# The low part of a weight as a negated copy and an accumulating DMA: a hybrid attention and state-space layer

## The chip, the cores and the metric

The kernel runs on one core of a Trainium2 chip. The metric is the device time of one execution in microseconds; three executions of the kernel before took 1957.34 to 1957.73 us, median 1957.66.

## What is computed

One layer serves a prompt of 1024 tokens and 8 samples of 16 tokens, 1152 tokens in all, with a model width of 1024. All tensors are float32. Cut to what matters:

```python
mod = jax.nn.silu(c) @ w_ada + b_ada
shift, scale, gate = jnp.split(mod[:, None, :], 3, axis=-1)
h = rms_norm(x, norm_g) * (1 + scale) + shift
proj = h @ w_in                      # q, k, v, z_att, z_ssd, xbc, dt, gates
q, k, v, z_att, z_ssd, xbc, dt_raw, gates = jnp.split(proj, IN_SPLITS, axis=-1)
o_att, k_st, v_st = attn_fn(rms_norm(q), rms_norm(k), v)       # 16 heads of 64, band of 8 chunks
att_branch = (o_att * jax.nn.silu(z_att)) @ w_att_proj
xbc, conv_new = causal_dwconv(xbc, conv_buf, conv_w, conv_b)   # 4 taps, 3072 channels
xs, bm, cm = jnp.split(jax.nn.silu(xbc), ...)
y, h_new = ssd_scan(xs, softplus(dt_raw + dt_bias), -jnp.exp(a_log), bm, cm, h0)   # 32 heads of 64
y = rms_norm_grouped((y + d_skip * xs) * jax.nn.silu(z_ssd))
merged = jax.nn.sigmoid(g_att) * att_branch + jax.nn.sigmoid(g_ssd) * (y @ w_ssd_proj)
out = x + gate * (merged @ w_out)
```

## The kernel before

Channels lie on the 128 partitions and tokens along the free axis, so an activation is a set of tiles of 128 x 1152. A projection is cut into jobs. A plain job has one weight block of 128 x 1024 float32 (eight tiles of 128 x 128, 512 KB) and computes 128 output channels for all tokens, in three groups of 384 tokens.

Matmuls run on float32r operands, and precision is kept by splitting each operand in two: a high part, rounded to float32r, and a low part, what is left of it. For each tile `mm` in `dense` (L436 to L445) gives TensorE three matmuls: high weights by high activations (L442), high by low (L443) and low by high (L445). So the high part of a weight is needed by the first matmul of a job and the low part by the third. A group of tokens has 24 matmuls and accumulates in one PSUM tile; the first two groups take turns in a pool of two (`psd`), in the state-space stage the third has a tile of its own (`pss`).

The weights arrive in order. `w_ahead` (L308) loads the next blocks by SyncE's DMA queue into two raw buffers, as soon as one is free. `w_split` (L316) makes the parts of one block: ScalarE copies the raw block into the high part (L334), VectorE subtracts the high part from the raw block into the low part (L335), and the raw buffer is given back. High and low parts of plain jobs live in four slots of `rarena` (`L_W`), that is two pairs: one for the job that runs and one for the next. `w_next` splits the next job's block while a job runs, if a pair of slots is free; otherwise `w_over` (L394) overwrites the pair of the running job piece by piece (L407, L408).

Jobs are numbered in the order of the weights: 0 to 15 are the attention stage's (`jobs_att[0]` is 16), 16 to 71 the 56 jobs of the state-space stage and its merge gates, and the last 32 (72 to 103) those of the tail: attention projection, state-space projection, output projection.

The state-space stage runs from about 640 to 1540 us of the profiled execution. Beside the dense jobs it has, for each of 16 pairs of heads, the convolution (`conv_gen`, L1229 to L1270), the decay masks (L1441 to L1459) and the scan itself (`main`, L1481 to L1616). ScalarE also evicts PSUM there (L1240, L1355, L1423). GpSimd does small copies and memsets for the convolution (L1232 to L1252), masked copies for the scan (L1515), and starts the DMAs that store results (L1253, L1356, L1540, L1590, L1616). While the attention stage ends, it also does the inverse square roots of its norms (L290 to L296, L960, L964).

The order of work: a Python generator traces the dense matmuls and, paced by a clock of its own, the other streams. A planner then lists each engine's instructions: among those that it expects to be ready it takes the one traced first, except that an instruction given to `keep_in_program_order` (`late` in the code) stays behind what was traced before it on its engine. On the chip each engine then runs its list in order and waits where an operand is not there. `w_split` has a parameter `keep`, which pins both its instructions when the next job is split inside the attention stage's last projections; job 16 is split that way.

Of the kernel before, what the change touches and what calls it, by code (L numbers as in the profile page):

```python
# [9 lines left out]
AF = mybir.ActivationFunctionType  # L10
ALU = mybir.AluOpType
# [110 lines left out]
def trunk_kernel(ctx: ExitStack, tc: tile.TileContext, h):  # L122
    nc = tc.nc
# [105 lines left out]
    def alloc(lay, tag, cols, cold=None):  # L229
        if lay is L_Q:  # L230
            try:
                return alloc(L_QR, tag, cols)
            except NoSlot:
                pass
        if lay is L_SSD and tag == "H":
            try:
                return Buf(qarena, qarena.alloc(L_QS, "ada", cols), cols)
            except NoSlot:
                pass
        if lay is L_Q or lay is L_QS:  # L240
            return Buf(qarena, qarena.alloc(lay, tag, cols), cols)
        if lay is L_W3 or lay is L_W7 or lay is L_VT or lay is L_VA:
            return Buf(varena, varena.alloc(lay, tag, cols), cols)
        if lay is L_H or lay is L_W or lay is L_WA or lay is L_QR or lay is L_ST:
            return Buf(rarena, rarena.alloc(lay, tag, cols, cold), cols)
        if (lay is L_SSD or lay is L_HEAD or lay is L_TAIL) and tag == "T" or lay is L_HEAD and tag == "Y":
            if v_open[0]:
                try:
                    return alloc(L_VT, "T", cols)
                except NoSlot:  # L250
                    pass
        return Buf(arena, arena.alloc(lay, tag, cols), cols)
# [46 lines left out]
    jobs, parts = [], []  # L299
# [8 lines left out]
    def w_ahead():  # L308
        while not hold[0] and loaded[0] < len(parts) and len(wraw) < 2:
            b = alloc(L_RAW, "raw", 1024)  # L310
            x = parts[loaded[0]]
            dma(b.ap[:, :x.shape[1]], x)
            wraw[loaded[0]] = b
            loaded[0] += 1

    def w_split(i, keep=lambda x: x, cold=None):  # L316

        n = len(jobs[i])
        if n == 4:
            return w_split_last(i, keep)  # L320
        if i not in wsplit:
            lay = L_W3 if n == 3 else L_WA if 0 < i < jobs_att[0] else L_W
            hi = alloc(lay, "w", n * 1024, cold)
            try:
                lo = alloc(lay, "w", n * 1024, cold)
            except NoSlot:
                hi.free()
                raise
            wsplit[i] = [hi, lo, 0]
        hi, lo, j = wsplit[i]  # L330
        w_ahead()
        b = wraw.pop(jobs[i][j])
        c = slice(j * 1024, (j + 1) * 1024)
        keep(nc.scalar.activation(hi.r[:, c], b.ap, AF.Copy))  # L334
        keep(nc.vector.tensor_tensor(lo.r[:, c], b.ap, hi.ap[:, c], ALU.subtract))  # L335
        b.free()
        wsplit[i][2] = j + 1
        w_ahead()

    def w_split_last(i, keep):  # L340

        n = NQL
        if i not in wsplit:
            hi = alloc(L_W7, "w", 7 * n)
            wsplit[i] = [hi, alloc(L_W7, "w", 7 * n), 0]
        hi, lo, j = wsplit[i]
        if j == 3:
            row = alloc(L_WA, "w", 1024)
            wsplit[i].append(row)
        w_ahead()  # L350
        b = wraw.pop(jobs[i][j])
        pieces = [(hi.r, hi.ap, lo.r, 2 * j * n, 0, 2 * n if j < 3 else n)]
        if j == 3:
            pieces.append((row.r, row.ap, row.r[:, n:], 0, n, n))
        for h_, f_, l_, o, r, w in pieces:
            keep(nc.scalar.activation(h_[:, o:o + w], b.ap[:, r:r + w], AF.Copy))
            keep(nc.vector.tensor_tensor(l_[:, o:o + w], b.ap[:, r:r + w], f_[:, o:o + w], ALU.subtract))
        b.free()
        wsplit[i][2] = j + 1
        w_ahead()  # L360
# [4 lines left out]
    def get_w(i):  # L365
        while w_left(i):
            w_split(i)
        return wsplit[i][:2]

    def w_wait(i):  # L370
        while w_left(i):
            try:
                w_split(i)
            except NoSlot as x:
                blocked[0] = str(x)
                yield None
        return wsplit[i][:2]

    def w_next(i, keep=lambda x: x):
        if w_left(i + 1):  # L380
            try:
                w_split(i + 1, keep, "q")
            except NoSlot:
                pass
# [37 lines left out]
    jobs_att = [len(jobs)]  # L422
# [99 lines left out]
    for k in range(KT):  # L522
        b = alloc(L_START, "T", NT)
# [200 lines left out]
    for k in range(KT):  # L724
        if k == 0:
# [22 lines left out]
            for i in range(3):  # L748
# [3 lines left out]
                b = wraw[1 + i] = alloc(L_RAW, "raw", 1024) if i < 2 else alloc(L_START, "T", 1024)  # L752
# [1172 lines left out]
```

## Time and profile before

| | |
|---|---|
| median of three runs | 1957.66 us |
| profiled execution, span | 1955.7 us |
| TensorE matmul busy | 1938.3 us, 99% |
| TensorE weight load busy | 1859.4 us, 95% |
| VectorE busy | 1168.5 us, 60% |
| ScalarE busy | 776.4 us, 40% |
| GpSimd busy | 323.5 us, 17% |
| granted TensorE clock | 1.00 in all slices |
| DMA | 238.62 MB, mean 122 GB/s |

The table shows one execution as the hardware profiler saw it. An engine's busy time leaves out what it waits. A matmul's end is modelled, so the share of TensorE says that it was hardly ever without an instruction, not that its array was full. The profile's views used below are the engine table, the chain of work that ended last, the stretch table (busy time of each engine between two times), the list of waits, the groups of instructions by line, the timeline of one engine, and the DMA starts with their time to landing.

### The profile page before, as it was taken

How to read it: one execution, taken by the hardware profiler on the slowest of the kernel's cores; microseconds unless marked ns; L12 is line 12 of the kernel's file. 1: busy time of each engine (PE TensorE's matmuls, PEld its weight loads, DVE VectorE, ACT ScalarE, POOL GpSimd, SP SyncE). 2: the span in 40 equal slices, each digit the busy share in tenths (PEclk: the TensorE clock that was granted, in tenths of full speed). 3: DMA queues.
4: the chain of work that ended last, by engine and by line, in shares of the span. 5: the costliest groups of instructions: out<-in, count | busy, mean ns of one | idle time of the engine just before them, and what ended most of it. 6: DMA issues, size and time to landing. Idle time of an engine off the chain costs nothing.

```text
span 1955.7 us, 35068 instructions
## 1 busy us (share of the span) xinstructions
PE 1938.3 (99%) x14091; PEld 1859.4 (95%) x14091; DVE 1168.5 (60%) x2441; ACT 776.4 (40%) x1589; POOL 323.5 (17%) x624
## 2 busy tenths in 40 slices
PE   7999999999999999999999999999999999999999
PEld 5999999899998999999999999999999999999999
DVE  7455555556555765757566666576674334777732
ACT  8444444445444557344454434345351301111200
POOL 0312213122131201212212221122212100000000
PEclk9999999999999999999999999999999999999999
DMA  9124244232432325433333333332337642331241
GB/s 367 60 81 131 86 132 131 90 122 88 131 112 96 112 88 160 128 112 110 95 132 129 106 103 114 117 118 91 117 118 291 234 140 92 104 104 56 86 143 52
DMA packets 81209, 238.62 MB, mean 122 GB/s; under 512 B 14284, under 2 KB 15320, under 8 KB 81048
## 3 DMA queue, kind: packets, MB, share of 16 engines
q1 hardware_dynamic: 72088, 207.74, 32.7%
q0 software_dynamic: 8960, 28.65, 3.8%
q8 instruction: 111, 1.82, 0.4%
q14 instruction: 50, 0.41, 0.1%
HBM read 192.70 MB, written 43.66 MB: 121 GB/s over the span
## 4 chain that ended last, share of the span: by engine, by line
PE 96%; DVE 1%; ACT 1%; DMA 1%; issue 0%; SPq 0%
PE d L442 13%; PE d L443 13%; PE d L445 13%; PE s L442 5%; PE s L445 5%; PE s L443 5%; PE d L508 5%; PE d L506 5%; PE d L507 5%; PE g L1043 3%; PE g L1066 3%; PE g L1553 2%; PE s L1122 2%; PE g L1526 1%; PE g L1573 1%; PE g L1122 1%
## 5 line engine op out<-in xcount | busy, mean ns | idle before, releaser
L442 PE MATMUL d<-rarena 128*128 128x384 f32 x1520 | 517.4, 340 | 0.3 <-ACT arena L1355 0.3
L445 PE MATMUL d<-rarena 128*128 128x384 f32 x1520 | 511.4, 336 | 0.0
L443 PE MATMUL d<-rarena 128*128 128x384 f32 x1520 | 511.0, 336 | 0.0
L442 PEld LDWEIGHTS d<-rarena 128*128 128x128 f32 x1520 | 285.6, 188 | 4.6 <-issue 2.3
L443 PEld LDWEIGHTS d<-rarena 128*128 128x128 f32 x1520 | 285.6, 188 | 2.8 <-issue 2.4
L445 PEld LDWEIGHTS d<-rarena 128*128 128x128 f32 x1520 | 285.5, 188 | 1.1 <-issue 0.9
L334 ACT ACTIVATE rarena<-arena 128x1024 fp32r<-128x1024 f32 x92 | 97.5, 1060 | 314.1 <-PE s L443 226.2
L442 PE MATMUL s<-rarena 128*128 128x384 f32 x640 | 216.7, 339 | 0.0
L443 PE MATMUL s<-rarena 128*128 128x384 f32 x640 | 214.2, 335 | 0.0
L445 PE MATMUL s<-rarena 128*128 128x384 f32 x640 | 214.1, 334 | 0.0
L508 PE MATMUL d<-va_att,rarena 128*128 128x384 f32 (+1 forms) x559 | 195.0, 349 | 0.0
L506 PE MATMUL d<-va_att,rarena 128*128 128x384 f32 (+1 forms) x559 | 193.9, 347 | 0.0
L507 PE MATMUL d<-va_att,rarena 128*128 128x384 f32 (+1 forms) x559 | 191.0, 342 | 0.0
L335 DVE TENSOR_TENSOR rarena<-arena,rarena 128x1024 fp32r<-128x1024 f32 x92 | 113.2, 1230 | 82.7 <-ACT rarena L334 82.4
L1031 ACT ACTIVATE arena<-arena 128x640 f32<-128x640 f32 (+2 forms) x144 | 101.4, 706 | 138.0 <-DVE arena L1140 99.7
L442 PEld LDWEIGHTS s<-rarena 128*128 128x128 f32 x640 | 120.3, 188 | 1.0 <-issue 1.0
L443 PEld LDWEIGHTS s<-rarena 128*128 128x128 f32 x640 | 120.3, 188 | 0.0
L445 PEld LDWEIGHTS s<-rarena 128*128 128x128 f32 x640 | 120.1, 188 | 0.0
L508 PEld LDWEIGHTS d<-va_att,rarena 128*128 128x128 f32 x559 | 105.5, 189 | 3.9 <-issue 2.7
L1263 DVE SCALAR_TENSOR_TENSOR arena<-arena 128x1176 f32<-128x1176 f32 x66 | 99.9, 1514 | 15.5 <-ACT arena L1260 14.2
L506 PEld LDWEIGHTS d<-va_att,rarena 128*128 128x128 f32 x559 | 105.2, 188 | 3.1 <-issue 1.2
L507 PEld LDWEIGHTS d<-va_att,rarena 128*128 128x128 f32 x559 | 105.2, 188 | 1.0 <-issue 0.4
(345 smaller groups left out, 3212.9 us busy)
## 6 DMA issues: line engine op xcount, KB each, us to landing
arena<-in_wall_dram SPq DMA_DIRECT2D x85, 512.0 KB, 3.9
arena<-in_kc_dram SPq DMA_DIRECT2D x64, 256.0 KB, 4.2
arena<-in_vc_dram SPq DMA_DIRECT2D x64, 256.0 KB, 3.4
arena<-acs_d SPq DMA_DIRECT2D x19, 576.0 KB, 3.8
gate_d<-arena POOLq DMA_DIRECT2D x48, 192.0 KB, 2.5
arena<-y_d SPq DMA_DIRECT2D x15, 576.0 KB, 5.6
arena<-in_wssd_dram SPq DMA_DIRECT2D x16, 512.0 KB, 4.1
arena<-in_wada_dram SPq DMA_DIRECT2D x15, 512.0 KB, 8.9
```

Of the source, the lines that this page charges most:

```text
L334: keep(nc.scalar.activation(hi.r[:, c], b.ap, AF.Copy))
L335: keep(nc.vector.tensor_tensor(lo.r[:, c], b.ap, hi.ap[:, c], ALU.subtract))
L442: nc.tensor.matmul(ps, hi.r[:, wc], kh.r[:, tok], start=k == 0, stop=False)
L443: nc.tensor.matmul(ps, hi.r[:, wc], kl.r[:, tok], start=False, stop=False)
L445: nc.tensor.matmul(ps, lo.r[:, wc], kh.r[:, tok], start=False, stop=k == nk - 1)
L506: nc.tensor.matmul(ps, kh.r[:, tok], wh, start=j == 0, stop=False)
L507: nc.tensor.matmul(ps, kh.r[:, tok], wl, start=False, stop=False)
L508: nc.tensor.matmul(ps, kl.r[:, tok], wh, start=False, stop=j == KT - 1)
L1031: nc.scalar.activation(p, p, AF.Exp, bias=sm_[:, 4 + e:5 + e], scale=-1.0, accum_out=sm_[:, 6 + e:7 + e])
L1043: nc.tensor.transpose(ps[:, s * P:(s + 1) * P], p[:, (j + s) * P:(j + s + 1) * P], ident)
L1122: late(nc.tensor.matmul(banks[k][e][:, o:o + w], x.r[hs, qs], y.r[hs, kk], start=i == 0, stop=i == 2))
L1263: nc.vector.scalar_tensor_tensor(yc, r.ap[:, j:j + n], w4[:, i, j:j + 1], yc, ALU.mult, ALU.add)
```

## The change

In `w_split`, for a block of the state-space stage (jobs 16 to 71), the low part is no longer VectorE's subtraction. ScalarE copies the high part, multiplied by -1, into the low part's slot, and a DMA started from GpSimd's queue adds the weights to it; it reads them from DRAM once more (`parts[...]` is the block that the raw buffer was loaded from). The jobs of the other stages, and the piecewise path in `w_over`, are as before. From here on lines have numbers four higher.

```diff
         keep(nc.scalar.activation(hi.r[:, c], b.ap, AF.Copy))
-        keep(nc.vector.tensor_tensor(lo.r[:, c], b.ap, hi.ap[:, c], ALU.subtract))
+        if jobs_att[0] <= i < len(jobs) - 32:
+            keep(nc.scalar.activation(lo.r[:, c], hi.ap[:, c], AF.Copy, scale=-1.0))
+            keep(nc.gpsimd.dma_start(lo.r[:, c], parts[jobs[i][j]], accum_op=ALU.add))
+        else:
+            keep(nc.vector.tensor_tensor(lo.r[:, c], b.ap, hi.ap[:, c], ALU.subtract))
         b.free()
```

## Rows read from the trace of the kernel before

**Rows 1.** The page: span; busy us (share of the span) and instructions by engine
```profile
span 1955.7 us, 35068 instructions
PE 1938.3 (99%) x14091; PEld 1859.4 (95%) x14091; DVE 1168.5 (60%) x2441; ACT 776.4 (40%) x1589; POOL 323.5 (17%) x624
```
**Rows 2.** The page: the chain that ended last, shares of the span by engine
```profile
PE 96%; DVE 1%; ACT 1%; DMA 1%; issue 0%; SPq 0%
```
**Rows 3.** Stretch table: stretch, length, busy us by engine, clock, DMA share, GB/s
```profile
640.00:1540.00 900.00, 897.53 (x6552) 878.49 (x6551) 578.17 (x1021) 393.78 (x807) 182.56 (x345) 1.00 0.38 126
```
**Rows 4.** Waits of TensorE, 640 to 1540: waiter <- releaser: total us, times, longest
```profile
PE g L1481 <- DVE arena L1269: 1.8, 2, 1.4
...
PE d L442 <- ACT arena L1355: 0.3, 1, 0.3
```
**Rows 5.** Groups by line: form, count | busy us, mean ns | idle before, releaser
```profile
L334 ACT ACTIVATE rarena<-arena 128x1024 fp32r<-128x1024 f32 x92 | 97.5, 1060 | 314.1 <-PE s L443 226.2
...
L335 DVE TENSOR_TENSOR rarena<-arena,rarena 128x1024 fp32r<-128x1024 f32 x92 | 113.2, 1230 | 82.7 <-ACT rarena L334 82.4
```
**Rows 6.** Timeline of ScalarE: start, us, form; high parts of jobs 16, 21, 22, 29, 55, 60
```profile
644.52 1.06 ACT L334 ACTIVATE rarena<-arena 128x1024 fp32r<-128x1024 f32 x1
...
735.09 1.06 ACT L334 ACTIVATE rarena<-arena 128x1024 fp32r<-128x1024 f32 x1 [0.26 <-PE s L443]
...
765.55 1.06 ACT L334 ACTIVATE rarena<-arena 128x1024 fp32r<-128x1024 f32 x1
...
875.57 1.05 ACT L334 ACTIVATE rarena<-arena 128x1024 fp32r<-128x1024 f32 x1
...
1278.28 1.04 ACT L334 ACTIVATE rarena<-arena 128x1024 fp32r<-128x1024 f32 x1
...
1351.59 1.05 ACT L334 ACTIVATE rarena<-arena 128x1024 fp32r<-128x1024 f32 x1
```
**Rows 7.** Timeline of TensorE: the third matmul of the same jobs
```profile
650.14 0.42 PE L445 MATMUL d<-rarena 128*128 128x384 f32 x1
...
757.60 0.35 PE L445 MATMUL d<-rarena 128*128 128x384 f32 x1
...
776.67 0.34 PE L445 MATMUL d<-rarena 128*128 128x384 f32 x1
...
884.42 0.33 PE L445 MATMUL d<-rarena 128*128 128x384 f32 x1
...
1286.12 0.33 PE L443 MATMUL d<-rarena 128*128 128x384 f32 x1
1286.30 0.33 PE L445 MATMUL d<-rarena 128*128 128x384 f32 x1
...
1361.29 0.33 PE L445 MATMUL d<-rarena 128*128 128x384 f32 x1
```
**Rows 8.** DMA starts of GpSimd: count, KB each, median us to landing
```profile
gate_d<-arena POOLq DMA_DIRECT2D x48, 192.0 KB, 2.5
...
out_hs_dram<-qa_ssd POOLq DMA_DIRECT2D x8, 512.0 KB, 2.9
```
**Rows 9.** Line 312, loads of weights of 512 KB, 740 to 1540
```profile
DMA to landing us min/median/max: 3.5/4.1/7.9
```
**Rows 10.** Line 1356, GpSimd's DMA starts, 740 to 1540: ns min/median/max
```profile
L1356 POOL DMA_DIRECT2D gate_d<-arena x45: 539/544/627, 752.5 to 1536.3; - x45
```
**Rows 11.** Timeline of GpSimd, around 646 and 871
```profile
645.91 3.69 POOL L291 TENSOR_TENSOR arena<-arena 128x16 f32<-128x16 f32 x1
...
871.48 0.54 POOL L1590 DMA_DIRECT2D y_d<-arena  x1 [15.50 <-DVE arena L1586]
```
**Rows 12.** Timeline of TensorE, 651 to 659, other work than the projection
```profile
651.01 0.71 PE L1043 MATMUL g<-arena 128*128 128x128 f32 x5
...
653.60 3.50 PE L1066 MATMUL g<-arena 128*64 128x128 f32 x60
...
657.02 1.30 PE L1202 MATMUL g<-arena 128*32 128x128 f32 x40
```

## The prediction

> **What bounds the kernel now.** I read the engine table of the page first. Of a span of 1955.7 us TensorE is busy for 1938.3, 99%; VectorE for 1168.5 and ScalarE for 776.4 [rows 1]. The chain that ended last agrees: 96% of it is TensorE, 1% VectorE [rows 2]. These are means over stages, so the second view is the stretch table of the stage that is changed. From 640 us, where the stage's first projection falls, to 1540 us TensorE is busy for 897.53 of 900.00 us [rows 3]. The reader is to see two things there. All idle time of TensorE in the stage is 900.0 - 897.5 = 2.5 us, so that is the most that relief on any other engine can give back. And nothing but TensorE is near its limit: VectorE has 578 of 900 us, ScalarE 394, GpSimd 183. The view of waits names what ended that idle time: VectorE's L1269 with 1.8 us, in two waits; ScalarE's eviction L1355 with 0.3 us, in one [rows 4]. The subtraction L335 is not among the releasers.
>
> The profiled execution stands 2.0 us under the median (1957.66 - 1955.7): what lies around the span. I sum on the span and add that.
>
> **The change, part by part.** Jobs are numbered as in the code; 16 to 71 are in the new branch. Jobs 17 to 19 take the other path (w_over), which keeps VectorE, so 53 jobs change.
>
> Removed: 53 subtractions at 1230 ns [rows 5], 65 us of VectorE. TensorE doesn't wait for them, so this is worth what part of the 2.5 us of idle time they caused: between -2.5 and 0. I take 0, because ScalarE's new copy stands at the same points of the same stretches.
>
> Added on ScalarE: 53 copies. The nearest row is the copy of the same size that makes the high part, 1060 ns [rows 5]: 56 us, which brings ScalarE in the stage from 394 to about 450 of 900 us. Behind each copy stand on ScalarE the evictions of PSUM, and for those TensorE waits. The cover is the second PSUM buffer of the projections: a group is 24 matmuls, whose starts are 0.17 us apart (1286.12 to 1286.30 [rows 7]), about 4.1 us, and an eviction that starts 1.1 us later still ends inside that. Without that cover the price would be 53 x 1.06 = 56 us; with it, 0 to 2 us. I take 0.5, since the one eviction in the waits is late by 0.3 us only [rows 4].
>
> Added on GpSimd's queue: 53 DMA starts. A start there takes 0.54 us, at most 0.63 [rows 10], 29 us in all on an engine with 183 of 900. The start waits for ScalarE's copy, and behind it are queued the stores (L1253, L1356, L1540, L1590, L1616), the halo memsets and copies, and the masks L1515 for TensorE's L1598. As the copy follows the high part directly, they wait about 1 us more; none of them releases TensorE in the waits [rows 4]. Cost: 0. On SP's queue nothing is added; the raw buffer is freed by the high part alone, so the next load may start some 1.2 us earlier. That is worth nothing, as no projection waits for it.
>
> The price that decides is the landing of the accumulating DMA, because now the low part is ready when it has landed. The trace shows no such DMA. Below: a plain store of 512 KB from GpSimd's queue lands in 2.9 us, median [rows 8]. Above: the slowest load of 512 KB of these weights from SP's queue lands in 7.9 us; its median is 4.1 us [rows 9]. The DMA has this load's bytes to fetch and 512 KB of the low part to read as well. From 192 KB in 2.5 us to 512 KB in 2.9 us, a store costs 0.4 us per 320 KB [rows 8], so the second read is about 0.6 us. I take 4.1 + 0.6 = 4.7 us, near the median load, and keep 2.9 and 7.9 (with the second read about 8.5) for the range.
>
> For the adding in the DMA the Trainium skill has a rule, in "Collectives: The Full Stack", section "The bandwidth ceiling: the fold count and why AG ≠ RS ≠ AR": a transfer that adds reads two sources through one ring and so runs at half the rate of a copy. By it the landing would be at most twice the median load, an estimate of 8.2 us, and the sum that of the first rival at its far end. No run here shows it yet.
>
> How long may it take? The end of the high part (L334) against the third matmul of the job (L445, the first that needs the low part) gives each job's room. For 49 of the 53 jobs it is 10.1 us or more: job 22 has 776.67 - 766.61 = 10.1, job 21 with 757.60 - 736.15 = 21.5 the most [rows 6, 7]. This is by construction: the high part waits for the slots that the job before the last one held (most of ScalarE's idle time ahead of L334, 226.2 us, ended with TensorE's L443 [rows 5]) and so starts as the job before begins. From the room go 1.06 us for the copy and up to 0.6 us for an instruction that runs on GpSimd just then: 8.4 us and more are left, against 4.7. They cost nothing. Four jobs have less [rows 6, 7]:
> job 55: 1286.30 - 1279.32 = 7.0, left 5.3; job 29: 884.42 - 876.62 = 7.8, left 6.1; job 60: 1361.29 - 1352.64 = 8.7, left 7.0. All three above 4.7. If one of them meets the slowest landing it costs 1 to 3 us; I take 0.4 for the three.
> Job 16: 650.14 - 645.58 = 4.6. Its copy would end at 646.7, but GpSimd is then in the power step L291 from 645.91 for 3.69 us [rows 11], so the DMA starts at 649.6 and lands at 654.3: 4.2 us after TensorE's need.
>
> Whether these 4.2 us are lost depends on the planner, which lists TensorE's instructions by what it expects to be ready. If it sees the late landing it can list other work first; L1043 (0.71) and L1202 (1.30) follow in 651 to 658, and L1066 with 3.50 as soon as its copies are there [rows 12]. Ends: 0 and 4.2. I take that the first two are moved, 2.0 us, and 2.2 are lost.
>
> Sum: 0 (VectorE) + 0.5 (evictions) + 0.4 (three tight jobs) + 2.2 (job 16) = +3.1 us. Span 1958.8, time 1960.8.
>
> **The rivals.** (1) Job 16 uncovered, landing 5 to 8 us. The mechanism is one wait of TensorE on the DMA at the stage's first projection, with the three tight jobs behind it. At 5 us it costs 4.5 and nothing else: 1962. At 8 us: 7.5 + 2.7 + 1.9 + 1.0 = 13: 1971. It is slower from the point where more than 3.9 us stay uncovered. For it: GpSimd is really busy there for 3.69 us, and the pinned order of this one job leaves the DMA no way past. Against it: other TensorE work stands right behind.
> On a delay of the start the Trainium skill says, in "SBUF — State Buffer", section "Who interferes with whom", that VectorE in its two-port modes locks GpSimd out while it writes descriptors, and that queues like SP's don't suffer. It speaks against moving this work from VectorE to GpSimd's queue; by it some landings would be later by one VectorE instruction, which is a time inside this rival. The trace doesn't show it: with VectorE busy for 64% of the stage [rows 3], 45 starts lie between 0.539 and 0.627 us [rows 10].
> (2) The add runs far below the copying rate, landing 10 us or more. Then the ordinary jobs pay too: 24 of 53 have less than 13 us of room. At 10 us I sum some 25 us over nine jobs, time 1983; at 12 us some 56, 2013. For it: no row shows what an add costs. Against it: 10 us is over twice the median load.
> (3) Head of GpSimd's queue. A start that the planner lists behind a store waits with it; the store of y at 871 stood there for 15.50 us [rows 11]. A job with 8.4 us left would lose 7. Two to four of these: 1972 to 1985. Against it: the listed order has been near to what happened in every stage, with TensorE never waiting.
> (4) All is hidden and VectorE's relief gives back the idle time: up to -2.5, 1955.2 to 1957.7. It can hardly go past that, as TensorE's own work is the same.
> That the change doesn't do what it says: only if the planner kept L335 for these jobs, which the branch rules out; three jobs of 56 are outside.
>
> **How the numbers follow.** A measurement of this kernel can tell about 0.2%, 3.9 us, from no change: from 1953.7 to 1961.6 is "the same". Forecast 1960.8 (own range 1957.7 to 1961.6): 0.46. Rival 1: 0.30. Rival 2: 0.10. Rival 3: 0.06. Rival 4: 0.08, of which 0.03 for an order of TensorE's work that happens to be better by more than 0.2%. So faster 0.03, same 0.51, slower 0.46. The range takes in the forecast, rival 1, half of rival 3 and rival 4 but for its tail: 1955.5 to 1978, leaving out about 0.16.
>
> **What would show it.** L335 on rarena falls from 92 to 39 instructions; a second ScalarE row of 1060 ns follows L334; GpSimd has 53 DMA rows into rarena of about 0.55 us. Landing of these: median 4.7 right, 8 rival 1, 10 rival 2. TensorE's waits on a DMA into rarena: one of 0 to 4 us near 650 by the forecast; 5 to 8 there, and near 884, 1286 and 1361, by rival 1; many of 1 to 4 through the stage by rival 2; a few of 5 or more after a long GpSimd wait by rival 3. I would be wrong in the cover if TensorE stays 99.9% busy with landings of 8 us and more, and in the 0 for VectorE if its idle time goes down.

## The result and the profile after

The changed kernel took 1961.34 us, median of 8 executions (1959.05 to 1965.93); the kernel before, measured beside it, 1957.5 us (1956.1 to 1958.33). The ratio is 1.0023, 95% interval 1.0013 to 1.0034. The profiled execution has a span of 1959.5 us against 1955.7 [rows 1].

The page of the changed kernel, engine table and chain of work that ended last, answers to [rows 1, 2]:

```profile
span 1959.5 us, 35155 instructions
...
PE 1940.4 (99%) x14091; PEld 1860.7 (95%) x14091; DVE 1103.7 (56%) x2388; ACT 823.1 (42%) x1642; POOL 347.3 (18%) x677
...
PE 91%; DMA 4%; issue 2%; ACT 2%; DVE 1%; POOL 0%; SPq 0%; POOLq 0%; ACTq 0%
```

The exchange itself is as written: VectorE has 53 instructions fewer and 65 us less, ScalarE and GpSimd 53 more each. In the chain DMA went from 1% to 4% and TensorE from 96% to 91% [rows 2]. The stretch table of the stage and TensorE's waits in it answer to [rows 3, 4]:

```profile
640.00:1540.00 900.00, 895.15 (x6526) 875.35 (x6525) 512.36 (x968) 439.79 (x859) 204.59 (x395) 1.00 0.58 156
```

```profile
PE d L449 <- DMA rarena<-in_wall_dram: 4.3, 4, 3.1
PE g L1485 <- DVE arena L1273: 0.5, 1, 0.5
```

TensorE's idle time in the stage went from 2.5 to 4.9 us, and its makeup is another: four waits of the third matmul (L449, before L445) on the new DMA, the longest 3.1 us, and 0.5 us on L1273, where L1269 (now L1273) with 1.8 us and L1355 with 0.3 us stood before. Two columns at the end of the stretch table show the second fetching of the 53 blocks: DMA share 0.58 for 0.38, 156 GB/s for 126. The DMA issues on the page, and the view of line 337 (duration of its starts, and issue to landing):

```profile
rarena<-in_wall_dram POOLq DMA_DIRECT2D x53, 512.0 KB, 6.7
```

```profile
L337 POOL DMA_DIRECT2D rarena<-in_wall_dram x53: 873/900/1078, 648.5 to 1526.9; - x53
...
DMA to landing us min/median/max: 5.4/6.7/11.4
```

A landing takes 6.7 us, median, and a start 0.90 us against 0.54 for a store [rows 10]. TensorE's timeline gives the other three waits on it, at jobs 29, 60 and 70; the longest, at job 55, stands further down:

```profile
881.48 0.44 PE L449 MATMUL d<-rarena 128*128 128x384 f32 x1 [0.45 <-DMA rarena<-in_wall_dram]
...
1365.26 0.44 PE L449 MATMUL d<-rarena 128*128 128x384 f32 x1 [0.66 <-DMA rarena<-in_wall_dram]
...
1524.86 0.44 PE L449 MATMUL d<-rarena 128*128 128x384 f32 x1 [0.18 <-DMA rarena<-in_wall_dram]
```

**Where the time went.** Setting the starts of the jobs of both traces side by side gives the ledger. Up to job 16 the changed kernel is 0.3 us ahead. Between job 16 and job 25 (650 to 821 us) it gains 3.3 us: all the idle time that TensorE had there before is gone, and some more. These are the first matmuls of the two jobs, before (L442) and after (L446):

```profile
649.76 0.33 PE L442 MATMUL d<-rarena 128*128 128x384 f32 x1
...
824.58 0.33 PE L442 MATMUL d<-rarena 128*128 128x384 f32 x1
```

```profile
649.51 0.34 PE L446 MATMUL d<-rarena 128*128 128x384 f32 x1
...
821.03 0.33 PE L446 MATMUL d<-rarena 128*128 128x384 f32 x1
```

Then it loses: 0.7 at job 29, 0.7 at job 50 (with the wait of L1485, 0.5 us), 4.9 at job 55, 0.95 at job 60, 0.45 at job 70. Together -0.3 - 3.3 + 7.7 = +4.1, and the spans differ by +3.8; the rest is gained behind job 72.

Job 55 is more than half of the loss. Its way can be followed on three engines. ScalarE's timeline (high part L334, negated copy L336):

```profile
1275.78 1.04 ACT L334 ACTIVATE rarena<-arena 128x1024 fp32r<-128x1024 f32 x1
1276.73 0.68 ACT L1457 ACTIVATE va_ssd<-va_ssd,arena 128x128 f32<-128x128 f32 x2
1277.32 0.36 ACT L1247 ACTIVATE arena<-s 128x256 f32<-128x256 f32 x1
1277.58 0.26 ACT L1248 ACTIVATE arena<-s 128x128 f32<-128x128 f32 x1
1277.74 1.27 ACT L1457 ACTIVATE va_ssd<-va_ssd,arena 128x128 f32<-128x128 f32 x4
1278.91 1.05 ACT L336 ACTIVATE rarena<-rarena 128x1024 fp32r<-128x1024 f32 x1
1279.86 1.36 ACT L1264 ACTIVATE arena<-arena 128x1176 f32<-128x1176 f32 x1
```

GpSimd's timeline, the start of the DMA, and TensorE's, the second and the third matmul of the job:

```profile
1281.55 0.90 POOL L337 DMA_DIRECT2D rarena<-in_wall_dram  x1 [2.54 <-ACT arena L1264]
```

```profile
1284.10 0.34 PE L447 MATMUL d<-rarena 128*128 128x384 f32 x1
1287.50 0.69 PE L449 MATMUL d<-rarena 128*128 128x384 f32 x1 [3.06 <-DMA rarena<-in_wall_dram]
```

The high part ends at 1276.82; the copy starts 2.1 us later, behind the eight other instructions of four rows; it ends at 1279.96; the DMA starts 1.6 us after that, in the trace behind ScalarE's L1264; it lands 5.90 us later, at 1287.45, and TensorE goes on at 1287.50. And the wait has a tail. The stretch table of what follows (its last columns: granted clock, DMA share, GB/s):

```profile
1287.50:1290.00 2.50, 2.50 (x8) 2.50 (x9) 1.74 (x3) 2.50 (x4) 0.31 (x2) 0.50 0.30 82
1290.00:1293.00 3.00, 3.00 (x17) 3.00 (x16) 0.16 (x1) 0.50 (x1) 0.88 (x1) 0.87 0.89 331
```

From the end of the wait of 3.06 us TensorE was granted 0.50 of its clock, 1.2 of 2.4 GHz, until about 1290.8 (0.87 in the second stretch is 0.8 us at 0.50 and the rest at 1.00). That isn't idle time in any view: 8 matmuls in 2.50 us, where 0.17 us apiece [rows 7] would have given 14. Half of 3.3 us is 1.6 us, and 3.1 + 1.6 = 4.7 is the 4.9 of the ledger but for 0.2. A stretch of 3.4 us at half clock takes about 0.001 from the mean clock of an execution of 1960 us. Of the eight executions only the shortest (1959.05 us) has a mean of 1.000, the profiled one and four others 0.999 and two 0.998; so most of them, but not all, seem to have such a stretch. Where it lies in the others no profile shows.

### The profile page after: what moved, and what is told of

It is laid out like the page before. It is cut to its first block, busy times and chain, and to the rows that moved or that the text cites. A ratio compares the mean times of both kernels' runs of the same rounds, so it can differ in the third digit from the quotient of the medians.

```text
span 1959.5 us, 35155 instructions
## 1 busy us (share of the span) xinstructions
PE 1940.4 (99%) x14091; PEld 1860.7 (95%) x14091; DVE 1103.7 (56%) x2388; ACT 823.1 (42%) x1642; POOL 347.3 (18%) x677
## 4 chain that ended last, share of the span: by engine, by line
PE 91%; DMA 4%; issue 2%; ACT 2%; DVE 1%; POOL 0%; SPq 0%; POOLq 0%; ACTq 0%
PE d L446 12%; PE d L449 12%; PE d L447 12%; PE d L512 5%; PE d L510 5%; PE d L511 5%; PE s L446 5%; PE s L449 5%; PE s L447 5%; PE g L1047 3%; PE g L1070 3%; PE s L1126 2%; PE g L1557 2%; DMA rarena<-in_wall_dram 2%; PE g L1530 1%
## 5 line engine op out<-in xcount | busy, mean ns | idle before, releaser
L446 PE MATMUL d<-rarena 128*128 128x384 f32 x1520 | 518.5, 341 | 0.0
L449 PE MATMUL d<-rarena 128*128 128x384 f32 x1520 | 511.7, 337 | 4.3 <-DMA rarena<-in_wall_dram 4.3
L447 PE MATMUL d<-rarena 128*128 128x384 f32 x1520 | 512.0, 337 | 0.0
L449 PEld LDWEIGHTS d<-rarena 128*128 128x128 f32 x1520 | 286.0, 188 | 6.6 <-DMA rarena<-in_wall_dram 5.6
L446 PEld LDWEIGHTS d<-rarena 128*128 128x128 f32 x1520 | 286.1, 188 | 5.9 <-issue 4.1
L447 PEld LDWEIGHTS d<-rarena 128*128 128x128 f32 x1520 | 286.1, 188 | 0.9 <-issue 0.5
L334 ACT ACTIVATE rarena<-arena 128x1024 fp32r<-128x1024 f32 x92 | 97.3, 1058 | 311.2 <-PE s L447 219.9
L446 PE MATMUL s<-rarena 128*128 128x384 f32 x640 | 216.9, 339 | 0.0
L449 PE MATMUL s<-rarena 128*128 128x384 f32 x640 | 214.2, 335 | 0.0
L447 PE MATMUL s<-rarena 128*128 128x384 f32 x640 | 214.1, 334 | 0.0
L1267 DVE SCALAR_TENSOR_TENSOR arena<-arena 128x1176 f32<-128x1176 f32 x66 | 95.3, 1444 | 48.0 <-ACT arena L1264 42.6
L446 PEld LDWEIGHTS s<-rarena 128*128 128x128 f32 x640 | 120.2, 188 | 1.1 <-issue 1.0
L447 PEld LDWEIGHTS s<-rarena 128*128 128x128 f32 x640 | 120.3, 188 | 0.2 <-issue 0.2
L449 PEld LDWEIGHTS s<-rarena 128*128 128x128 f32 x640 | 120.1, 188 | 0.2 <-issue 0.2
L964 POOL TENSOR_SCALAR arena<-arena 128x16 f32<-128x16 f32 (+1 forms) x24 | 5.1, 212 | 485.1 <-DVE arena L941 484.5
```

The costliest lines, as they stand in the source:

```text
L446: nc.tensor.matmul(ps, hi.r[:, wc], kh.r[:, tok], start=k == 0, stop=False)
L447: nc.tensor.matmul(ps, hi.r[:, wc], kl.r[:, tok], start=False, stop=False)
L449: nc.tensor.matmul(ps, lo.r[:, wc], kh.r[:, tok], start=False, stop=k == nk - 1)
L1267: nc.vector.scalar_tensor_tensor(yc, r.ap[:, j:j + n], w4[:, i, j:j + 1], yc, ALU.mult, ALU.add)
```

## The experiments

Each edit is against the changed kernel. Kernels were run in three sets, with the kernel before beside each set: 1957.18 us (runs e1 to e4), 1957.6 us (e5 to e8) and 1957.25 us (e9 to e11).

**Without the addition (e1).** The low part stays the negated high part; the DMA is left out.

```diff
             keep(nc.scalar.activation(lo.r[:, c], hi.ap[:, c], AF.Copy, scale=-1.0))
-            keep(nc.gpsimd.dma_start(lo.r[:, c], parts[jobs[i][j]], accum_op=ALU.add))
```

> The accumulating DMA is left out: the low part stays the negated high part, so the low weights are not added in the state-space stage; VectorE's subtraction stays removed and ScalarE's copy stays. Landing theory (the loss is TensorE's waits on the DMA's landing in jobs 29, 55, 60 and 71, some 7 us with the half clock behind them, against a gain of about 3.3 us in 650 to 805 us from VectorE's freed time): no such waits, 1954 us, 1953.3 to 1955.3. ScalarE theory (53 copies ahead of the evictions make the loss): still 1960 to 1962. Traffic theory (the second read of the weights slows other loads): 1954 too.

Measured: 1955.26 us, ratio 0.9989 (0.9980 to 0.9999). TensorE waits 0.44 us in the whole stage. ScalarE has its 53 copies here too, so these cost nothing that shows; the DMA is what costs. The list of TensorE's waits has one line:

```profile
PE g L1046 <- DVE arena L1039: 0.4, 2, 0.3
```

**A DMA that writes and doesn't add (e2).** Same bytes into the same slots from the same queue, without the addition.

```diff
-            keep(nc.gpsimd.dma_start(lo.r[:, c], parts[jobs[i][j]], accum_op=ALU.add))
+            keep(nc.gpsimd.dma_start(lo.r[:, c], parts[jobs[i][j]]))
```

> The DMA only writes the weights into the low part and doesn't add, so the low part is wrong in the state-space stage; queue, bytes from DRAM and starts are the same. If the add makes the landing (second read of the low part): median landing 4.1 to 4.9 us instead of 6.7, the wait of job 55 down from 3.1 to about 1.3 us, the others gone, time 1956 to 1958. If GpSimd's start and the load itself make it: landing 6 to 7 us, start still 0.90 us on GpSimd, time 1960 to 1962. Traffic theory: as the second.

Measured: 1956.72 us, ratio 0.9999 (0.9990 to 1.0008). TensorE's waits, and the view of line 337:

```profile
PE d L449 <- DMA rarena<-in_wall_dram: 1.9, 1, 1.9
```

```profile
L337 POOL DMA_DIRECT2D rarena<-in_wall_dram x53: 542/548/760, 648.2 to 1521.5; - x53
...
DMA to landing us min/median/max: 3.8/5.1/10.1
```

Of the four waits one is left, that of job 55, and behind it the clock stayed at 1.00. This profile is of the shortest of the ten executions (1955.40 us, mean clock 1.000); five of the ten have a mean clock of 0.999, so behind the same wait others may have had the half clock. The landing is above the 4.1 to 4.9 us that I expected. The addition lengthens it by 6.7 - 5.1 = 1.6 us, of which the start itself is 0.35 (0.90 against 0.55). That is enough to make jobs 29, 60 and 70 late: here they land 1.2, 1.2 and 1.0 us before the need. The second reading of the weights is all here too (157 GB/s in the stage against 156), so that traffic by itself isn't the loss.

**Three of the four jobs with waits keep the subtraction (e3).** I gave the fourth the number 71; in the trace it is job 70 that waits, 0.18 us, and job 71's low part lands 3.6 us before its need. So jobs 29, 55 and 60, which waited, and 71, which didn't, are taken out here, and job 70 keeps the DMA. The same holds for the number 71 in the other expectations.

```diff
-        if jobs_att[0] <= i < len(jobs) - 32:
+        if jobs_att[0] <= i < len(jobs) - 32 and i not in (29, 55, 60, 71):
```

> Jobs 29, 55, 60 and 71 keep VectorE's subtraction, the other 49 have the change. Landing theory: the four waits go, the gain at the start of the stage stays: 1955 us, 1953.5 to 1956.5, unless the new order makes another job tight, which the waits on the DMA would show. ScalarE theory: 49 of 53 copies are still there, so 1960 to 1962. Traffic theory: the same, 1960 to 1962.

Measured: 1955.67 us, ratio 0.9995 (0.9986 to 1.0004). No wait on a DMA is left, with 49 adding DMAs of 7.2 us, median, still there; job 70's lands 0.3 us before its need. What TensorE waits for is L1273:

```profile
PE g L1485 <- DVE va_ssd L1273: 1.6, 2, 1.4
```

The span fell by 1959.5 - 1953.6 = 5.9 us. The loss is that of a few jobs with little room, jobs 29, 55 and 60 above all, not of the 53.

**Only those four, 29, 55, 60 and 71 (e6).**

```diff
-        if jobs_att[0] <= i < len(jobs) - 32:
+        if i in (29, 55, 60, 71):
```

> Only jobs 29, 55, 60 and 71 have the change. Landing theory: they are late by their own chain (high part, copy, start, landing), so the waits are there without the other 49, and the early gain is not: 1960 to 1965 us, waits of TensorE on the DMA of 3 to 5 us in all. Rival (they are late because the other 49 DMAs and copies stand in the same queues): landing under 5.5 us, waits under 1 us in all, 1957 to 1958.5.

Measured: 1960.3 us, ratio 1.0013 (1.0004 to 1.0022). TensorE's waits:

```profile
PE d L449 <- DMA rarena<-in_wall_dram: 3.2, 2, 1.9
PE g L1485 <- DVE arena L1273: 2.2, 2, 1.7
```

With four DMAs alone on the path (landing 5.7 us, median) two of them still come late, 1.9 and 1.3 us, at jobs 29 and 55: the other 49 transfers aren't what makes them late; their own chain of copy, start and landing is. Job 60's lands 0.6 us before its need, job 71's 4.5. The clock stayed at 1.00 behind both waits. And without the other jobs the waits of before on L1273 are all there again, 2.2 us: the early gain is gone too. The profiled execution, 1961.61 us, has besides 0.50 of the clock from 29.8 to 33.2 us, long before the first changed job, so its span is not the price of the four jobs alone.

**The first ten blocks alone (e4): jobs 16 and 20 to 28.**

```diff
-        if jobs_att[0] <= i < len(jobs) - 32:
+        if jobs_att[0] <= i < 29:
```

> Only jobs 16 and 20 to 28 (ten blocks, 640 to 860 us) have the change. If VectorE's freed time at the start of the stage gives the gain: 1954.2 us (1953.5 to 1955), TensorE's idle time in 640 to 810 down from 2.5 to about 0. If the gain of 3.3 us there was one execution's chance: 1957 to 1958.

Measured: 1954.03 us, ratio 0.9985 (0.9977 to 0.9994). The early gain stands by itself, with 0.28 us of idle time in the stage. This is the time that I expected if VectorE's freed time gave the gain; the runs that follow show that it fits another cause as well.

**The same ten with VectorE adding (e5, and once more e11).** VectorE has its ten instructions back; only ScalarE's copy is new. The condition is that of e4, and besides:

```diff
-            keep(nc.gpsimd.dma_start(lo.r[:, c], parts[jobs[i][j]], accum_op=ALU.add))
+            keep(nc.vector.tensor_tensor(lo.r[:, c], b.ap, lo.ap[:, c], ALU.add))
```

> As the kernel with the ten early blocks (jobs 16 and 20 to 28), but the weights are added to ScalarE's negated copy by VectorE instead of the DMA, so VectorE has its 10 instructions back and ScalarE keeps its 10 copies. If VectorE's freed time gives the gain of some 3 us at the start of the stage: the gain goes, 1956 to 1959 us, with TensorE's idle time in 640 to 810 us back at 2 us or more. If another order of TensorE's work or ScalarE's copy gives it: 1953.5 to 1955.

Measured: 1954.89 us, ratio 0.9987 (0.9979 to 0.9996). My expectation fell: VectorE's relief was taken back and the gain stayed. But the profiled execution, 1957.43 us, was the longest of the eleven, with 1.48 us of waiting on L1273, so it couldn't show why the others were shorter. Hence the same kernel again:

> The ten blocks of jobs 16 and 20 to 28 with ScalarE's negated copy and VectorE's addition, once more, for another profile. If the waits of its first profile (1.48 us on L1273 at 756 us, 0.8 us in the scan at 773 to 777) belong to the program, the span is 1955 to 1956 and they are there again, and the shorter times of its other executions stay without a cause; if they were those of one execution, TensorE is idle for under 1 us from 640 to 1540 us and the span is 1952 to 1953.5.

Measured: 1955.06 us, ratio 0.9991 (0.9982 to 1.0000), with a span of 1952.6 us in the profile and 0.6 us of idle time in the stage; no wait on L1273. So the waits of the first profile don't belong to every execution of this program; its longest here is 1957.3 us, near that of the first profile.

**Only jobs 20 to 24 (e8).** These are the jobs whose subtractions stand in the stretch of the early gain.

```diff
-        if jobs_att[0] <= i < len(jobs) - 32:
+        if 20 <= i < 25:
```

> Only jobs 20 to 24 (blocks made from 715 to 795 us) have the change. If the gain sits where VectorE's subtraction stood on the chain of 750 to 805 us: all of it, 1953.5 to 1955 us. If it is spread over the stage's first 200 us: 1955 to 1957.

Measured: 1957.09 us, ratio 0.9998 (0.9990 to 1.0007). That is in neither range that I gave. No gain; L1485 waits 1.1 us on L1273, and TensorE 0.8 us on the DMA of job 22, which lands in time in the changed kernel. What was left of e4 was jobs 25 to 28, behind the stretch of the gain, and job 16, ahead of it. So the last question was put to job 16 alone, and to the others without it.

**Only job 16 (e9).**

```diff
-        if jobs_att[0] <= i < len(jobs) - 32:
+        if i == 16:
```

> Only job 16 gets the negated copy and the accumulating DMA; the other 52 keep VectorE's subtraction. Theory (the 3.3 us gained between 650 and 805 us come from the other order of TensorE's work that job 16's late low part leads to): job 17 starts some 4 us later as in the changed kernel, the waits on L1273 near 756 and 793 us are gone, and the time is 1953.5 to 1955.5. Rival (VectorE's freed time in jobs 20 to 28 is what clears those waits): they stay, 1.5 to 2.5 us, and the time is 1956.5 to 1958.5, that of the kernel before.

Measured: 1953.47 us (1953.06 to 1954.25), ratio 0.9980 (0.9972 to 0.9989): the shortest of all kernels here. The stretch table says that TensorE hasn't any idle time left in the stage, while VectorE is as busy as before (580 against 578 us [rows 3]):

```profile
640.00:1540.00 900.00, 900.00 (x6572) 882.48 (x6571) 580.21 (x1022) 399.10 (x810) 183.77 (x346) 1.00 0.39 127
```

TensorE's timeline at the start of job 16, from its second matmul (L447) to its third (L449); the DMA lands at 653.79:

```profile
649.27 0.42 PE L447 MATMUL d<-rarena 128*128 128x384 f32 x1
649.53 0.60 PE L988 MATMUL g<-arena 128*128 128x128 f32 x4
649.97 0.71 PE L1047 MATMUL g<-arena 128*128 128x128 f32 x5
650.61 3.50 PE L1070 MATMUL g<-arena 128*64 128x128 f32 x60
654.03 1.30 PE L1206 MATMUL g<-arena 128*32 128x128 f32 x40
655.26 0.45 PE L449 MATMUL d<-rarena 128*128 128x384 f32 x1
```

The planner has put all of the other work of [rows 12] (L1043, L1066, L1202, four lines higher here) between the two matmuls. The low part lands 1.5 us before it is needed, and this work is done some 3 us earlier than before. The effect at 790 us: VectorE's convolution step and the matmul that it released, in the kernel before,

```profile
792.46 1.21 DVE L1269 SCALAR_TENSOR_TENSOR arena<-arena 128x1024 f32<-128x1024 f32 x1
...
793.81 0.63 PE L1481 MATMUL g<-arena 128*128 128x128 f32 x4 [1.45 <-DVE arena L1269]
```

and the same two in this kernel:

```profile
784.66 1.23 DVE L1273 SCALAR_TENSOR_TENSOR arena<-arena 128x1024 f32<-128x1024 f32 x1 [0.74 <-ACT arena L1269]
```

```profile
788.86 0.81 PE L1485 MATMUL g<-arena 128*128 128x128 f32 x6
```

The step now ends 3.0 us before the matmul; before, 0.14 us ahead of a matmul that had waited 1.45 us for it.

**Jobs 20 to 28 without job 16 (e10).**

```diff
-        if jobs_att[0] <= i < len(jobs) - 32:
+        if 20 <= i < 29:
```

> Jobs 20 to 28 get the negated copy and the accumulating DMA, job 16 and all from 29 on keep the subtraction. Theory (job 16's change makes the early gain): job 20 starts some 5.5 us earlier and the time is 1956 to 1958, as in the run with jobs 20 to 24. Rival (VectorE's freed time makes it): waits on L1273 near 756 and 793 us gone, the time 1953.5 to 1955.5, as in the run with job 16 and 20 to 28.

Measured: 1957.34 us, ratio 1.0002 (0.9994 to 1.0011). TensorE's waits:

```profile
PE g L1485 <- DVE arena L1273: 1.3, 1, 1.3
PE d L449 <- DMA rarena<-in_wall_dram: 0.9, 1, 0.9
```

The wait on the DMA is again that of job 22; taken off, it would leave less than 1 us of the 3.3. So nine subtractions fewer on VectorE (568 us busy) give little or nothing; one subtraction fewer, the right one, gives all of it. The gain of the change comes from the order of TensorE's work that job 16's late low part led to. It isn't the only order with a gain: in e1 and e11 job 17 starts when it did before and job 20 some 5.5 us earlier, and no wait on L1273 is left. But that order by itself doesn't give it: job 20 is as early in e8, in e10 and in the profile of e5, with waits of 1.1, 1.3 and 1.5 us on L1273. What makes the difference wasn't tried apart; in e11 it can't be VectorE's relief, since VectorE has as many instructions as before.

**The negated copy from the raw block, ahead of the high part (e7).** It was meant to start the DMA a copy earlier.

```diff
+        if jobs_att[0] <= i < len(jobs) - 32:
+            keep(nc.scalar.activation(lo.r[:, c], b.ap, AF.Copy, scale=-1.0))
         keep(nc.scalar.activation(hi.r[:, c], b.ap, AF.Copy))
         if jobs_att[0] <= i < len(jobs) - 32:
-            keep(nc.scalar.activation(lo.r[:, c], hi.ap[:, c], AF.Copy, scale=-1.0))
             keep(nc.gpsimd.dma_start(lo.r[:, c], parts[jobs[i][j]], accum_op=ALU.add))
```

> All 53 blocks have the change, but ScalarE makes the negated copy from the raw block (rounded the same way) and ahead of the high part, so that the DMA can start 1.3 us earlier or more and the high part 1.1 us later. Landing theory: waits of jobs 29, 60 and 71 (0.2 to 0.7 us) gone, that of job 55 from 3.1 to under 1.5, no half clock behind it: 1953.5 to 1956.5 us. ScalarE theory: the same 53 copies, 1960 to 1962.

Measured: 1967.58 us, ratio 1.0057 (1.0044 to 1.0069). It failed twice over. ScalarE's timeline (L336 is the high part here, L335 the negated copy) shows that the planner turned the two round again, as in 52 of 53 jobs:

```profile
760.79 1.05 ACT L336 ACTIVATE rarena<-arena 128x1024 fp32r<-128x1024 f32 x1
...
762.11 1.05 ACT L335 ACTIVATE rarena<-arena 128x1024 fp32r<-128x1024 f32 x1
```

So at these 52 jobs the DMA still stands behind both copies, while the raw buffer is now held until the second copy has read it. Landings grew, and six jobs waited (16, 21, 29, 39, 55 and 60):

```profile
DMA to landing us min/median/max: 5.9/7.8/10.8
```

```profile
PE d L450 <- DMA rarena<-in_wall_dram: 9.5, 6, 3.0
```

Where the trace gives the next weight's load, it starts 0.3 us ahead of the adding DMA, where it stood 1.6 us ahead in the changed kernel. That the two are slower for it is likely, but wasn't tried by itself. The early gain is gone here too: job 25 starts 1.4 us later than in the kernel before. With e3 it fits that the landing decides at the jobs with little room: at 7.8 us instead of 6.7 six jobs are late instead of four.

## Why the prediction came out as it did

1960.8 us was forecast, with 1957.7 to 1961.6 as its own range, and 1961.34 us measured, inside it. The loss is clear of noise (1.0013 to 1.0034). The mechanism, TensorE waiting on the landing of a few jobs, is the one that is seen. Its place and the sizes were not.

- **The landing: 4.7 us taken, 6.7 measured**, between the ends that I had kept (2.9 and 8.5). The failing step is the estimate "4.1 + 0.6". e2 splits it: a plain load on this queue takes 5.1 us, not the 4.1 of SP's queue [rows 9], and the addition another 1.6, not 0.6. Of the rule in the Trainium skill, "Collectives: The Full Stack", section "The bandwidth ceiling: the fold count and why AG ≠ RS ≠ AR", a doubled landing didn't show: 6.7 against 5.1 is a factor of 1.3 at this size. Its direction holds. The section states the half rate for the adding step of a ring collective of three or more participants, so carrying it to a DMA of one core was my own step.
- **The start: 0.54 to 0.63 us taken, 0.90 measured.** The price was taken from stores [rows 10]; the accumulating form costs 0.35 us more in the same slots (e2: 0.55). Against the lock that the Trainium skill describes in "SBUF — State Buffer", section "Who interferes with whom", no start shows one: of 53 none took more than 1.08 us, with VectorE busy for 512 of 900 us. The lock is stated there for VectorE's two-port modes, and the profile doesn't tell VectorE's mode, so this isn't a test of the rule.
- **"The copy follows the high part directly" failed.** At 39 of the 53 jobs it starts about 0.3 us behind, but at jobs 29, 55 and 60 it came 2.1, 2.1 and 1.75 us behind, with evictions (L1247, L1248) and decay masks (L1457) listed between, as the timeline of job 55 shows. From the start of the DMA to the end of TensorE's work ahead of the third matmul 5.8, 2.9 and 5.5 us were left at jobs 29, 55 and 60, where I had written 6.1, 5.3 and 7.0: too much by 0.3, 2.4 and 1.5 us. At job 29 the high part ended earlier against the matmul than before (a room of 9.2 us for 7.8), which made up for most of the copy's delay. The landings of the three were 6.2, 5.9 and 6.1 us.
- **The three tight jobs: 0.4 us taken, about 6.6 measured** (0.7, 4.9 and 0.95, with job 70 0.45 more, which met the slowest landing, 11.4 us, beside a load of 11.9 us). This is the term that was mis-sized most. The points above make up the waits of jobs 29 and 60, 0.45 and 0.66 us; at job 55 1.6 us of the lost room lie between copy and start, and the half clock after the wait comes on top, which I hadn't thought of.
- **Job 16: 2.2 us taken as lost, nothing lost.** The DMA's start at 648.5 came even earlier than the 649.6 forecast; it landed in 5.55 us, at 654.05, 3.9 us after the need of the kernel before, but the third matmul stood at 655.71. I had named the work that could be moved ahead (L1043, L1066, L1202) and let the planner move two of the three; it moved all.
- **VectorE's relief: 0 taken. This 0 is right, but not that the idle time stays.** The 2.5 us of idle time between job 16 and job 25 went, and about 0.8 more, by the new order of TensorE's work behind job 16 (e9, e10), to which I had given 0.03, as a part of rival 4, "for an order of TensorE's work that happens to be better by more than 0.2%". What the 0.8 are, which lie in no idle time, isn't told apart. They also break the bound that I drew from the idle time, 2.5 us at the most: job 16 alone (e9) made the span 1955.7 - 1951.3 = 4.4 us shorter, 0.7 of it ahead of job 16.
- **Evictions: 0.5 taken.** No wait of TensorE on an eviction is left (e1 has all copies and 0.44 us of idle time, on other causes); 0 would have been right. What the list didn't hold is the new wait on L1273 ahead of job 50, 0.5 us, which costs 0.7 in the ledger; e3 has waits on it too (1.6 us), e1 has none, and what places them stays open.

So the sum of +3.1 us is near the measured +3.8 by luck, because errors cancelled: 7.0 - 0.4 = 6.6 us too little for jobs 29, 55, 60 and 70 and 0.7 for job 50, against 2.2 too much for job 16, 3.3 for the early part and 0.5 for the evictions. With the 0.7 by which the stretches ahead of job 16 and behind job 72 were shorter, 3.1 + 7.3 - 6.0 - 0.7 is 3.7. Of the rivals, 1 was right in the landing and in the three tight jobs, and wrong in job 16, which it made the main loss; 2 fell (no landing median near 10 us); 3 doesn't show at the jobs that waited: ahead of job 55's start GpSimd stood idle for 2.54 us, and the profile puts the end of that down to ScalarE's L1264, not to a store. What the start waited for in the last 1.6 us stays open. The price of rival 3 left out the landing besides: 15.5 + 4.7 - 8.4 is 11.8 us, not 7.

## What to carry to other kernels

When a low part, a mask or any operand is moved to a DMA, the cost lies in the few jobs with the least room: list the room of each, and charge to it the waiting of every step on its engine, not only the durations of the steps. Here leaving four of 53 blocks as they were, three of them blocks that TensorE had waited for, took back the loss. And where a planner orders the work, one changed readiness can move the whole stage: a single block, job 16, gave 0.2%, while nine others at the same engines gave nothing that shows in the time; test such an edit block by block before it is explained by an engine's share.

## What the runs showed of the hardware

- After its wait of 3.06 us (job 55) TensorE had 0.50 of its clock for some 3.3 us more, so that the wait cost 1.6 times its length. The length alone doesn't decide: e7 has such a stretch (0.65 from 889 to 893 us) behind waits of 0.4 and 2.4 us close together, and none behind its single waits of 3.0 and 2.6 us; nor has the profiled execution of e2 behind 1.9 us. In e6 the clock is 0.50 from 29.8 to 33.2 us behind waits of 0.94 and 0.91 us, and the kernel before has these two waits too (0.95 and 0.91 us) and keeps 1.00. What decides stays open.
- An accumulating DMA of 512 KB from GpSimd's queue, DRAM into SBUF: start 0.90 us, landing 6.7 us, median of 53; the plain one 0.55 and 5.1 us.
- The stores of 192 KB on the same queue land in 4.7 us, median, in the changed kernel and in 2.5 before [rows 8], without a wait of TensorE behind them. With one added DMA (e9) it is 3.0, but without any (e1) 3.7, so that the new transfers alone don't explain it.
